# Other constants for the scheduler of an attention-and-retention block: the same work in another order of issue

## The chip, the cores and the metric

The kernel runs on one core of one Trainium2 chip. The metric is the device time of one execution in microseconds. "Before" was executed three times.

## The reference, cut to what matters

One decoder layer on x of 512 x 1024 in float32. The input is normalized and projected by one wide weight matrix. Of the parts, one mixer is sparse attention (8 heads in 2 key groups: a branch on compressed keys, one on selected blocks, one on a window, added with gates), the other is retention with 4 heads in chunks of 128. Both are gated, merged, and go through an output projection; a last normalization and the residual follow.

```python
def compress_blocks(kv, pe, w1, w2):
    ...
    return jax.nn.gelu(flat @ w1) @ w2
...
    kc = compress_blocks(k_cmp_raw, cmp_pe_k, cmp_w1_k, cmp_w2_k)
    vc = compress_blocks(v_cmp_raw, cmp_pe_v, cmp_w1_v, cmp_w2_v)
...
        o = g[..., 0:1] * o_c + g[..., 1:2] * o_s + g[..., 2:3] * o_w
...
    att = jnp.einsum('nihd,njhd->nhij', qc, kc) * decay_mask[None]
    o_inner = jnp.einsum('nhij,njhe->nihe', att, vc)
```

## The kernel before, in words

**Weights and matmuls.** A float32 product is made of three matmuls: every operand is split into a high part (rounded to the type fp32r) and a low part (the rest), and high x high, high x low and low x high are added up in PSUM. Weights come from HBM in loads of 512 KB into four `raw` slots (`load_next`, L442 and L445, on SyncE's queue SP). A co-routine, `splitter`, turns each load into two weight halves: `whi` is a copy on ScalarE (L224) or a cast on VectorE (L232), `wlo` a subtraction on VectorE (L236, in `split_lo`), in a ring of nine. A load can start when both low parts of the slot's former content have been made. L224, L236 and so on are lines of helpers, which record every operation of their kind.

**Stages.** x is transposed and normalized (`hTh`, `hTl`); then come the projections for attention (`tail_a`, `tail_c`, `tail_q`), at about 60 to 80 us the two `hidden` blocks of the key and value compressor with `compress` behind them, then the block Z and the gates, the ZR, QK and VR projections, a `pair` of two such blocks done with seven products in place of eight on sums of weights and of inputs, and the output blocks. Attention (`attention`, `att_unit`, `att_head`, `att_cmp`, `att_sum`, `att_out`) runs between the blocks on all engines: L983 is the fused mask and row maximum of one head and half of the keys' range, ACT takes the exponential behind it, and a transposition on TensorE (L278) and an eviction by ACT and VectorE follow. `zr_end` (L1198) takes a part of ZR out of its PSUM bank.

**Sums of weights.** The seven products need x with signs: `signed` (L608) scales each of eight slices by plus or minus the norm on ACT and stores them to DRAM tiles `s` with 20 DMAs on SP (L621). When all are done, `weight_sums` (L416) lets GpSimd (POOL) copy a `mark` (L419), and then issues six DMAs (four copies, L412, and adds, L410, which read what a copy or a store has written), and nineteen more behind a second `mark` (L423) once the first Z tile is there.

**The order of issue.** Every engine runs its own queue in order, so what stands in front of a slow or waiting instruction matters. The order is worked out when the kernel is built, by the class `Order`. Each piece of work is a co-routine with a priority; it yields the time from which it can go on. `Order` keeps a clock for TensorE (`now`) and one for each other engine, goes through the pieces by priority, and takes the first whose time, plus a hold, has come:

```python
w += LAG + (0.0 if c[0] == MAIN else MARGINS.get(c[3].__name__, MARGIN))
if e:
    w = max(w, self.eng[e] - SLACK)
if w <= self.now:
    best = c
    break
```

The main line (the blocks' matmuls) has the last priority. `MARGINS` (L36) holds, in nanoseconds, each kind of piece back beyond its time: a larger hold lets other pieces and the main line go first. Besides that there are fixed delays: `HOLD` (L732) and `HOLD_C` (L764) between the copies of the keys and their transposition, and `SIGN`, `SIGN_LAG` (L608, L613), the priority of `signed` and the time that it is held. Weight halves have a priority that moves:

```python
return lambda: 0 if p <= wanted[0] + (PSOON if p in pairp else SOON) else 4
```

A half that is needed within the next two (`SOON`), or in the part of the `pair` within `PSOON`, goes before everything, the others behind most of it.

Of the kernel before, what the change touches and what calls it, by code (L numbers as in the profile page):

```python
# [31 lines left out]
MAIN = 9  # L32
LAG, PE_LAG = 55.0, 60.0
TAIL = {"act": 110.0, "dve": 82.0, "pool": 45.0}
MARGIN = 50.0
MARGINS = {'att_cmp': 400.0, 'att_head': 100.0, 'att_out': 100.0, 'att_sum': 20.0, 'att_unit': 100.0, 'compress': 800.0, 'ga_split': 1000.0, 'gates': 1300.0, 'h_sums': 250.0, 'keep': 600.0, 'kept': 1300.0, 'qk_end': 400.0, 'ret': 0.0, 'ret_state': 150.0, 's_early': 1000.0, 's_late': 800.0, 'seven_end': 1000.0, 'split_lo': 100.0, 'splitter': 250.0, 'tail_a': 0.0, 'tail_c': 20.0, 'tail_m': 250.0, 'tail_o': 1300.0, 'tail_q': 20.0, 'tail_qk': 600.0, 'tail_yb': 250.0, 'tail_z': 20.0, 'x_split': 20.0, 'zr_end': 150.0}  # L36
SOON = 2
PSOON = 4
ISSUE = 8.0
SLACK = 700  # L40
WAKE = 7
SIGN, SIGN_LAG = 4, 22000.0
HOLD_C = 1000.0
EARLY = 1300.0
HOLD = 800.0
OSUMS = (1, 0, 0, 0, 1, 0, 0, 0)
FIRST, NEXT, BESIDE = 6, 19, 4000.0
DVE_BIAS = 500
# [2 lines left out]
class Order:  # L51
# [51 lines left out]
    def run(self):  # L103
        while self.cos:
            best = None
            for c in sorted(self.cos, key=lambda c: (c[0]() if callable(c[0]) else c[0], c[1])):
                w, e = c[2] if isinstance(c[2], tuple) else (c[2], None)
                if callable(w):
                    if not w():
                        continue  # L110
                    w = 0.0
                w += LAG + (0.0 if c[0] == MAIN else MARGINS.get(c[3].__name__, MARGIN))
                if e:
# [37 lines left out]
def block_kernel(ctx: ExitStack, tc, x, xT, x0s, ws, small, w2s, norm_post, rope_r, dmask, out):  # L151
# [283 lines left out]
    def load_next():  # L435
        i = len(raws)
        if i < len(loads):
            raw = rp.tile([P, 1024], FT, name="raw", tag="raw", bufs=NR)
            o, c, r = loads[i][0], 0, parts[2 * (i - NR) + 1][2] if i >= NR else 0.0
            for j, n in enumerate(loads[i][1]):  # L440
# [7 lines left out]
                if i + j == 0:  # L448
                    load_xT(0)
            raws.append((raw, e + (EARLY if 6 <= i < 16 else 0.0)))  # L450
            for fn in hook.get(i, ()):
# [66 lines left out]
    def rank(p):  # L518

        return lambda: 0 if p <= wanted[0] + (PSOON if p in pairp else SOON) else 4  # L520

# [61 lines left out]
    def load_xT(k):  # L583
        c0 = 0 if k else 256
        DMA.dma_start(xTf[k][:, c0:], xT[k * P:(k + 1) * P, c0:])
        xTr[k] = od.dma(P * (SEQ - c0) * 4)
# [111 lines left out]
    def keysT(kd, off, br, t, r):  # L698
        ps = yield from PT.get()
        yield r + PE_LAG  # L700
        for g in range(2):
            e = tr(ps[:, g * P:(g + 1) * P], kd[:, off + g * P:off + (g + 1) * P], ident, r)
        yield e, "act"
        v = ps[:, 0:256].rearrange("p (g c a) -> p g a c", g=2, a=2)
        sl = (slice(None), br, slice(None), slice(None), slice(t * 64, (t + 1) * 64))
        e = act(kA[sl], v, r=e)
        yield e, "dve"
        e = sub_split(kB[sl], v, kA[sl], e)
        PT.put(ps, e)
        return e  # L710
# [8 lines left out]
    def tail_a(t, ps, e, ring):  # L719
# [11 lines left out]
        NAT.put(kn, ev)  # L731
        yield e + HOLD  # L732
        yield from keysT(kd, 512, 0, t, e)
# [18 lines left out]
    def tail_c(t, ps, e):  # L752
# [10 lines left out]
        NAT.put(kn, ev)  # L763
        yield e + HOLD_C  # L764
        e = yield from keysT(kd, 0, 1, t, e)
# [1244 lines left out]
```

## Time and profile before

| | |
|---|---|
| median of 3 executions | 496.04 us (494.77 to 496.93) |
| the profiled execution | 496.11 us |
| its span | 494.3 us |
| granted clock of TensorE, mean | 0.994 |
| DMA | 98.75 MB, mean 200 GB/s |
| `raw` loads from the weights' stream | 73, of 512 KB |

The profile has a timeline of every engine (PE is TensorE, PEld its weight loads, DVE VectorE, ACT ScalarE, POOL GpSimd, SP the queue of SyncE). A row of the timeline has the start in us, the duration, engine, line, operation, output <- input, and in brackets the idle time in front and what ended it. A window's row has its length, the busy time of PE, PEld, DVE, ACT and POOL with the number of instructions, the granted clock of TensorE, the busy share of the DMA engines, and GB/s. PE's instructions overlap (a matmul of 512 columns is shown with 0.38 us but the next starts 0.22 behind it), so PE can be busy and still be late.

### The profile page before, as it was taken

What the parts mean: (1) busy time and instruction counts of PE and PEld (TensorE: products, weight loads), DVE (VectorE), ACT (ScalarE), POOL (GpSimd) and SP (SyncE); (2) the same over time, 40 slices, a digit from 0 to 9 for tenths busy, and PEclk for the clock granted to TensorE, in tenths of its full rate; (3) what the DMA queues carried; (4) which work ended last, traced back from release to release, by engine and by line L of the source; (5) the groups of instructions that cost most, each with busy time, mean ns of one, the idle gap of its engine ahead of it and who ended that gap; (6) DMA issues with size and microseconds to landing.
All of it is one profiled execution on the core that took longest, in us unless ns stands there. A gap on an engine that the chain in (4) does not pass through costs nothing.

```text
span 494.3 us, 7886 instructions
## 1 busy us (share of the span) xinstructions
PE 477.7 (97%) x2666; PEld 424.0 (86%) x2666; DVE 424.4 (86%) x996; ACT 323.3 (65%) x722; POOL 39.7 (8%) x66
## 2 busy tenths in 40 slices
PE   8999997999999999999999999999999999999993
PEld 7899876888788888887989878989889999988882
DVE  5789899989989988989798998878787867979886
ACT  5777678677869889983596684665445535538632
POOL 2103010023100210000100000001000000000010
PEclk9999998999999999999999999999999999999998
DMA  8937989779997899426466783630573736535814
GB/s 308 397 141 233 382 227 286 257 138 183 358 286 144 240 368 205 148 64 192 89 195 213 226 256 107 128 129 2 170 253 123 229 119 192 193 127 170 300 42 170
DMA packets 31080, 98.75 MB, mean 200 GB/s; under 512 B 3136, under 2 KB 6976, under 8 KB 30272
## 3 DMA queue, kind: packets, MB, share of 16 engines
q1 hardware_dynamic: 24576, 70.85, 42.7%
q0 software_dynamic: 6320, 27.26, 22.9%
q8 instruction: 21, 0.34, 0.3%
q10 hardware_dynamic: 144, 0.14, 0.1%
q14 instruction: 19, 0.16, 0.1%
HBM read 93.52 MB, written 31.98 MB: 254 GB/s over the span
## 4 chain that ended last, share of the span: by engine, by line
PE 84%; DVE 9%; ACT 2%; issue 2%; DMA 1%; DVEq 0%; POOLq 0%; POOL 0%; ACTq 0%
PE bank L272 67%; PE bank L1251 7%; PE bank L1745 7%; PE bank L278 4%; DVE wlo L236 3%; DVE words L236 2%; DVE arena_r L236 2%; DVE words L983 1%; ACT arena_r L224 1%; DVE words L249 1%; DMA words<-in_x_dram 1%; ACT whi L224 1%; ACT words L224 0%; DVE arena_r L249 0%; DVE whi L232 0%
## 5 line engine op out<-in xcount | busy, mean ns | idle before, releaser
L224 ACT ACTIVATE whi<-raw 128x512 fp32r<-128x512 f32 x175 | 105.3, 626 | 48.6 <-PE bank L272 37.0
L236 DVE TENSOR_TENSOR wlo<-raw,whi 128x512 fp32r<-128x512 f32 x188 | 122.7, 684 | 8.1 <-ACT whi L224 7.4
L272 PE MATMUL bank<-whi,hTh 128*128 128x512 f32 x192 | 72.6, 399 | 3.2 <-DVE arena_r L249 1.9
L272 PE MATMUL bank<-whi,hTl 128*128 128x512 f32 x192 | 69.7, 384 | 0.0
L272 PE MATMUL bank<-wlo,hTh 128*128 128x512 f32 x192 | 69.7, 384 | 0.0
L272 PE MATMUL bank<-arena_r 128*128 128x256 f32 (+2 forms) x328 | 68.2, 330 | 0.7 <-DVE stat L983 0.4
L224 ACT ACTIVATE arena_r<-bank 128x512 fp32r<-128x512 f32 (+3 forms) x104 | 49.2, 476 | 23.1 <-PE bank L278 22.0
L272 PE MATMUL bank<-arena_r,whi 128*128 128x512 f32 (+1 forms) x208 | 61.6, 372 | 0.0
L236 DVE TENSOR_TENSOR arena_r<-bank,arena_r 128x512 fp32r<-128x512 f32 (+3 forms) x104 | 55.8, 541 | 5.3 <-ACT arena_r L224 4.0
L224 ACT ACTIVATE words<-words,stat 128x128 f32<-128x128 f32 (+3 forms) x109 | 56.0, 545 | 6.6 <-DVE stat L236 4.2
L272 PEld LDWEIGHTS bank<-arena_r 128*128 128x128 f32 x328 | 51.7, 191 | 6.6 <-DVE stat L983 1.8
L272 PE MATMUL bank<-hTh,whi 128*128 128x512 f32 (+1 forms) x144 | 51.2, 356 | 0.0
L272 PE MATMUL bank<-hTh,wlo 128*128 128x512 f32 (+1 forms) x144 | 50.1, 348 | 0.9 <-DVE wlo L236 0.9
L272 PE MATMUL bank<-hTl,whi 128*128 128x512 f32 (+1 forms) x144 | 49.9, 347 | 0.0
L272 PEld LDWEIGHTS bank<-whi,hTh 128*128 128x128 f32 x192 | 36.8, 192 | 8.7 <-DVE arena_r L249 2.5
L272 PEld LDWEIGHTS bank<-arena_r,whi 128*128 128x128 f32 x208 | 39.1, 189 | 5.0
L272 PEld LDWEIGHTS bank<-whi,hTl 128*128 128x128 f32 x192 | 36.9, 192 | 5.4
L272 PEld LDWEIGHTS bank<-wlo,hTh 128*128 128x128 f32 x192 | 37.0, 192 | 4.1
L278 PEld LDWEIGHTS bank<-identr,shorts 128*128 128x128 f32 x268 | 30.1, 142 | 8.5 <-ACT words L224 1.7
L272 PE MATMUL bank<-arena_r,wlo 128*128 128x512 f32 x96 | 36.4, 379 | 0.0
L224 ACT ACTIVATE words<-words 128x512 f32<-128x512 f32 (+3 forms) x47 | 27.1, 581 | 10.1 <-DVE words L236 6.4
L278 PE MATMUL bank<-identr,shorts 128*128 128x128 f32 x268 | 32.2, 241 | 1.2 <-ACT words L224 1.0
(182 smaller groups left out, 888.0 us busy)
## 6 DMA issues: line engine op xcount, KB each, us to landing
raw<-in_stream_dram SPq DMA_DIRECT2D x73, 512.0 KB, 4.5
pair<-in_stream_dram POOLq DMA_DIRECT2D x6, 1024.0 KB, 13.7
t<-in_stream_dram POOLq DMA_DIRECT2D x6, 1024.0 KB, 17.5
out<-in_stream_dram POOLq DMA_DIRECT2D x6, 1024.0 KB, 17.1
words<-in_x_dram SPq DMA_DIRECT2D x8, 512.0 KB, 7.3
raw<-s SPq DMA_DIRECT2D x8, 512.0 KB, 3.7
raw<-pair SPq DMA_DIRECT2D x8, 512.0 KB, 4.6
raw<-t SPq DMA_DIRECT2D x8, 512.0 KB, 3.8
```

The source lines that it names most:

```text
L224: S.activation(o, i, func, **kw)
L236: (V if e == "dve" else G).tensor_tensor(o, a, b, op=op)
L249: V.scalar_tensor_tensor(o, a, s, b, op0=op0, op1=op1)
L272: T.matmul(ps, a, b, start=start, stop=stop)
L278: T.transpose(ps, a, idn)
L983: V.tensor_tensor_reduce(pv[:, b, :], sv[:, b, :], maskp[:, 512 - L:512], 1.0, -NEG, OP.add, OP.min, nm[:, b:b + 1])
L1251: T.matmul(ps[m], a, apart(b), start=n in first and s + j == 0, stop=n in last and s + j == 5, skip_group_check=True)
L1745: T.matmul(ps[m], a, apart(b), start=n in first and s + i == 0, stop=n in last and s + i == 5, skip_group_check=True)
```

## The change

The default hold stays (50), and 26 of the 29 holds by kind get other values; `PSOON` goes from 4 to 8, `SIGN` from 4 to 3, `SIGN_LAG` from 22000 to 19000, `HOLD_C` from 1000 to 300 and `HOLD` from 800 to 500. Nothing else is edited. The table in full is one line; of it, the kinds that the text speaks of:

```diff
-MARGINS = {'att_cmp': 400.0, 'att_head': 100.0, 'att_out': 100.0, 'att_sum': 20.0, ... 'compress': 800.0, ... 'gates': 1300.0, ... 'split_lo': 100.0, ... 'tail_c': 20.0, ... 'zr_end': 150.0}
+MARGINS = {'att_cmp': 50.0, 'att_head': 0.0, 'att_out': 1300.0, 'att_sum': 400.0, ... 'compress': 1300.0, ... 'gates': 800.0, ... 'split_lo': 20.0, ... 'tail_c': 250.0, ... 'zr_end': 1700.0}
...
-PSOON = 4
+PSOON = 8
...
-SIGN, SIGN_LAG = 4, 22000.0
-HOLD_C = 1000.0
+SIGN, SIGN_LAG = 3, 19000.0
+HOLD_C = 300
...
-HOLD = 800.0
+HOLD = 500
```

The changed kernel has the same number of matmuls, DMAs and POOL instructions; three copies go from VectorE to ScalarE. Three places of the queues:

VectorE, in the compressor's first `hidden` block. `wlo` is the low part of a weight half, `stat` holds the maxima of the heads, `bank_86` and `bank_87` their scores, and `words_128_...` is the compressor's activation (L983 with `stat` alone reads out the maximum). Before:

```order
L983 ISA words_512_131,stat_905<-bank_87,maskp 128x512
L983 ISA stat_905 128x1
L236 TENSOR_TENSOR words_128_1022<-bank_88,words_128_1023 128x128
L236 TENSOR_TENSOR words_128_1023<-words_128_1022 128x128
L245 TENSOR_SCALAR words_128_1023<-words_128_1023 128x128
L236 TENSOR_TENSOR words_128_1023<-words_128_1023,words_128_1022 128x128
L983 ISA words_512_132,stat_905<-bank_86,maskp 128x512
L983 ISA stat_905 128x1
L983 ISA words_512_133,stat_905<-bank_87,maskp 128x512
L983 ISA stat_905 128x1
L232 CAST whi<-raw 128x512
L236 TENSOR_TENSOR wlo<-raw,whi 128x512 x2
```

In the changed kernel, around the same two heads:

```order
L236 TENSOR_TENSOR wlo<-raw,whi 128x512
L236 TENSOR_TENSOR arena_r<-bank_88,arena_r 64x4x128 x2
L236 TENSOR_TENSOR wlo<-raw,whi 128x512 x2
L243 TENSOR_SCALAR words_512_115<-words_512_115,stat_884 128x512
L236 TENSOR_TENSOR wlo<-raw,whi 128x512
L983 ISA words_512_131,stat_885<-bank_87,maskp 128x512
L983 ISA stat_885 128x1
L983 ISA words_512_132,stat_885<-bank_86,maskp 128x512
L983 ISA stat_885 128x1
L236 TENSOR_TENSOR wlo<-raw,whi 128x512 x3
L236 TENSOR_TENSOR arena_r<-bank_88,arena_r 128x512
L236 TENSOR_TENSOR wlo<-raw,whi 128x512
```

Before, three heads and the activation stand together ahead of the cast and the two splits; now five splits stand ahead of the heads, and the activation comes later.

ScalarE, in `zr_end`, where `words_512_114` takes a quarter of the ZR block out of `bank_85`. Before:

```order
L224 ACTIVATE whi<-raw 128x512 x3
L224 ACTIVATE arena_r<-bank_89 128x4x128
L224 ACTIVATE whi<-raw 128x512 x3
L224 ACTIVATE words_512_114<-bank_85,rs_169 128x512
L224 ACTIVATE whi<-raw 128x512
```

In the changed kernel:

```order
L224 ACTIVATE whi<-raw 128x512 x3
L224 ACTIVATE words_512_129<-words_512_113 128x512
L224 ACTIVATE whi<-raw 128x512
L224 ACTIVATE words_512_114<-bank_85,rs_169 128x512
L224 ACTIVATE whi<-raw 128x512 x2
```

Directly ahead of that eviction stood three copies of weights, and now there stands one; two more have moved behind it.

GpSimd (POOL), where the sums of weights begin. `gate` is the gates' input of one tile of x (`tail_c`), `mark` the copy that waits for the signed x; the rows L412 copy, and the rows L410 add to what the copies and the stores of `s` have left. Before:

```order
L236 TENSOR_TENSOR gate<-words_512_126,cst 128x24
L236 TENSOR_TENSOR gate<-words_512_127,cst 128x24
L236 TENSOR_TENSOR gate<-words_512_126,cst 128x24
L236 TENSOR_TENSOR gate<-words_512_128,cst 128x24
L419 COPY mark<-words_512_115 128x1
L412 DMA pair_157<-in_stream_dram 128x2x1024
```

In the changed kernel:

```order
L236 TENSOR_TENSOR gate<-words_512_126,cst 128x24
L236 TENSOR_TENSOR gate<-words_512_127,cst 128x24
L236 TENSOR_TENSOR gate<-words_512_128,cst 128x24
L419 COPY mark<-words_512_115 128x1
L412 DMA pair_157<-in_stream_dram 128x2x1024
L412 DMA pair_159<-in_stream_dram 128x2x1024
L412 DMA pair_158<-in_stream_dram 128x2x1024
L412 DMA pair_160<-in_stream_dram 128x2x1024
L410 DMA s_148<-s_151 128x2x1024
L410 DMA pair_157<-in_stream_dram 128x2x1024
L236 TENSOR_TENSOR gate<-words_512_126,cst 128x24
```

One of the four rows of `gate` no longer stands ahead of `mark`; it follows two adds. On SP, three loads of weights that stood between the stores of the signed x now follow all of them.

More of the change, by code (lines that the diff above doesn't have):

```diff
@@ L34 @@
 TAIL = {"act": 110.0, "dve": 82.0, "pool": 45.0}
-MARGIN = 50.0
-MARGINS = {'att_cmp': 400.0, 'att_head': 100.0, 'att_out': 100.0, 'att_sum': 20.0, 'att_unit': 100.0, 'compress': 800.0, 'ga_split': 1000.0, 'gates': 1300.0, 'h_sums': 250.0, 'keep': 600.0, 'kept': 1300.0, 'qk_end': 400.0, 'ret': 0.0, 'ret_state': 150.0, 's_early': 1000.0, 's_late': 800.0, 'seven_end': 1000.0, 'split_lo': 100.0, 'splitter': 250.0, 'tail_a': 0.0, 'tail_c': 20.0, 'tail_m': 250.0, 'tail_o': 1300.0, 'tail_q': 20.0, 'tail_qk': 600.0, 'tail_yb': 250.0, 'tail_z': 20.0, 'x_split': 20.0, 'zr_end': 150.0}
+MARGIN = 50
+MARGINS = {'att_cmp': 50.0, 'att_head': 0.0, 'att_out': 1300.0, 'att_sum': 400.0, 'att_unit': 100.0, 'compress': 1300.0, 'ga_split': 1300.0, 'gates': 800.0, 'h_sums': 1000.0, 'keep': 100.0, 'kept': 50.0, 'qk_end': 250.0, 'ret': 20.0, 'ret_state': 0.0, 's_early': 0.0, 's_late': 1000.0, 'seven_end': 0.0, 'split_lo': 20.0, 'splitter': 250.0, 'tail_a': 20.0, 'tail_c': 250.0, 'tail_m': 800.0, 'tail_o': 20.0, 'tail_q': 50.0, 'tail_qk': 600.0, 'tail_yb': 20.0, 'tail_z': 50.0, 'x_split': 0.0, 'zr_end': 1700.0}
 SOON = 2
-PSOON = 4
+PSOON = 8
 ISSUE = 8.0
@@ L41 @@
 WAKE = 7
-SIGN, SIGN_LAG = 4, 22000.0
-HOLD_C = 1000.0
-EARLY = 1300.0
-HOLD = 800.0
+SIGN, SIGN_LAG = 3, 19000.0
+HOLD_C = 300
+EARLY = 1300
+HOLD = 500
 OSUMS = (1, 0, 0, 0, 1, 0, 0, 0)
```

## The prediction

> **What bounds the kernel now.** I read the page first: the busy rows and the chain that ended last.
>
> ```profile
> PE 477.7 (97%) x2666; PEld 424.0 (86%) x2666; DVE 424.4 (86%) x996; ACT 323.3 (65%) x722; POOL 39.7 (8%) x66
> ...
> PE 84%; DVE 9%; ACT 2%; issue 2%; DMA 1%; DVEq 0%; POOLq 0%; POOL 0%; ACTq 0%
> ```
>
> TensorE (PE) is the bound. The change takes no matmul away, so it can win only the 494.3 − 477.7 = 16.6 us in which PE isn't busy and what is hidden in matmuls that sit longer than they need. So I went through the span in windows of 10 us, to see where PE loses time. The six below hold 5.8 of the 16.6; most of the rest is the start and the end, where the order is the same.
>
> ```profile
> 60.00:70.00 10.00, 9.73 (x52) 7.82 (x50) 9.71 (x26) 8.35 (x17) 2.38 (x2) 1.00 0.83 262
> 70.00:80.00 10.00, 7.96 (x48) 6.02 (x47) 9.75 (x26) 7.24 (x15) 0.00 (x0) 1.00 1.06 249
> 80.00:90.00 10.00, 9.19 (x51) 8.14 (x52) 9.93 (x24) 10.00 (x24) 0.00 (x0) 0.83 0.83 303
> ...
> 130.00:140.00 10.00, 9.14 (x48) 7.69 (x47) 9.59 (x24) 7.27 (x14) 2.30 (x2) 1.00 1.03 359
> 220.00:230.00 10.00, 9.07 (x49) 7.31 (x47) 10.00 (x20) 4.74 (x10) 0.00 (x0) 1.00 0.57 190
> 290.00:300.00 10.00, 9.07 (x48) 7.53 (x46) 9.12 (x18) 5.61 (x11) 0.00 (x0) 1.00 0.77 253
> ```
>
> The columns are PE, weight loads, VectorE (DVE), ScalarE (ACT) and POOL busy, then clock, DMA share and GB/s. From 60 to 90 us PE loses 3.1 us by busy time, and in the same stretch DVE is busy for 29.4 of 30: the stage is DVE's. The other three windows lose just under 1 us each. Behind 302 us nothing is left to win: the chain is one run of matmuls.
>
> ```profile
> 349.27 100.83 PE bank L272 x621
> 450.10 33.68 PE bank L1745 x156
> ```
>
> **Term 1, the stage from 60 to 90 us.** PE is in the `hidden` blocks of the compressor here and waits for weight halves; DVE has the first attention heads (L983 head maxima) in its queue as well.
>
> ```profile
> 69.65 1.89 DVE L236 TENSOR_TENSOR wlo<-raw,whi 128x512 fp32r<-128x512 f32 x3
> 71.46 0.68 DVE L983 CUSTOM_DVE_ANT_0 words<-bank,maskp 128x512 f32<-128x512 f32 x1
> ...
> 72.07 1.28 DVE L236 TENSOR_TENSOR wlo<-raw,whi 128x512 fp32r<-128x512 f32 x2
> ...
> 76.42 0.69 DVE L983 CUSTOM_DVE_ANT_0 words<-bank,maskp 128x512 f32<-128x512 f32 x1
> ...
> 79.98 0.42 DVE L232 CAST whi<-raw 128x512 fp32r<-128x512 f32 x1
> 80.44 1.29 DVE L236 TENSOR_TENSOR wlo<-raw,whi 128x512 fp32r<-128x512 f32 x2
> ```
>
> ```profile
> 80.46 0.38 PE L272 MATMUL bank<-whi,arena_r 128*128 128x256 f32 x1 [0.74 <-DVE whi L232]
> 81.18 0.38 PE L272 MATMUL bank<-wlo,arena_r 128*128 128x256 f32 x1 [0.35 <-DVE wlo L236]
> ```
>
> From start to start a split `wlo` takes 0.60 us ((71.46 − 69.65)/3) and a head maximum 0.61 (72.07 − 71.46). Between 76.42 and 79.98 DVE does 3.56 us of work that PE doesn't wait for yet, and PE waits for the cast and the split behind it. These are the rows shown of DVE's order ahead of this text: three heads and the compressor's activation, then the cast and two splits. In the changed order the splits stand ahead, the heads are spread behind them, and the casts that DVE did for `whi` are ACT's. To price this I gave every row of both orders the mean start-to-start time of its form in the trace of before, and compared, for each place where a matmul waits for DVE, the sum of DVE rows up to what it waits for with the sum of PE rows up to the matmul. At the last split of the first `hidden` block that is 73.9 us of DVE against 72.0 of PE before, and 69.1 against 70.2 now. Over the stage the largest lead of DVE's sum falls from 2.95 to 0.30 us. With DVE as full as it is, PE's place moves by that difference, 2.65; the two `whi` waits of the rows above (0.74, and some of the 0.35) go to ACT, which isn't the bound, so I take 3.1 and keep 1.5 to 4.7 (4.7: all of the 3.1 us not busy, and the clock's loss in the rows below, 1.0 in the first and 0.6 in the second).
>
> ```profile
> 82.00:84.00 2.00, 2.00 (x10) 1.71 (x10) 2.00 (x6) 2.00 (x7) 0.00 (x0) 0.50 1.04 424
> 84.00:86.00 2.00, 2.00 (x12) 1.82 (x12) 1.97 (x6) 2.00 (x5) 0.00 (x0) 0.70 0.58 236
> ```
>
> After the thin microseconds from 70 on the granted clock drops to half. I count none of that 1.6 as gain by itself, since DVE's lead covers it: PE at full clock would have waited for DVE. [...]
>
> What ACT needs doesn't rise to the bound: its sum leads PE's by −8.25 us in this stage before and by −7.14 now, and it gets its weights late only if DMA is slow (second rival).
>
> **Terms 2 to 5.** At 132.8 us PE waits for a split that stands behind a chain on the compressed scores.
>
> ```profile
> 131.47 0.68 DVE L249 SCALAR_TENSOR_TENSOR words<-words,words 128x512 f32<-128x512 f32 x1
> 132.07 2.49 DVE L236 TENSOR_TENSOR wlo<-raw,whi 128x512 fp32r<-128x512 f32 x4
> ```
>
> ```profile
> 131.57 0.38 PE L272 MATMUL bank<-hTl,whi 128*128 128x512 f32 x1
> 132.81 0.48 PE L272 MATMUL bank<-hTh,wlo 128*128 128x512 f32 x1 [0.86 <-DVE wlo L236]
> ...
> 293.65 0.48 PE L272 MATMUL bank<-whi,hTh 128*128 128x512 f32 x1 [0.81 <-ACT words L224]
> ```
>
> A matmul of this size takes 33.68/156 = 0.216, so the first loses 132.81 − 131.57 − 0.22 = 1.02, and 0.1 in its own longer row. DVE's lead there is 2.6 before and −1.6 now, from 110 us of PE work to 160: gone, −1.1. The second, at 293.65, waits for an eviction that ACT took late, behind three copies.
>
> ```profile
> 291.36 1.66 ACT L224 ACTIVATE whi<-raw 128x512 fp32r<-128x512 f32 x3
> 292.92 0.68 ACT L224 ACTIVATE words<-bank,rs 128x512 f32<-128x512 f32 x1
> ```
>
> This is the place shown of ACT's order (`words_512_114`). Two copies have moved behind it, 2 × 0.52 (292.92 − 291.36 = 1.56 for three) = 1.04: −1.0. Two more gaps have the shape matmul, ACT, DVE, matmul on one bank, and that stays:
>
> ```profile
> 229.92 0.48 PE L272 MATMUL bank<-whi,hTh 128*128 128x512 f32 x1 [0.76 <-DVE arena_r L249]
> ...
> 301.02 0.48 PE L272 MATMUL bank<-whi,hTh 128*128 128x512 f32 x1 [1.15 <-DVE arena_r L249]
> ```
>
> At the first DVE does another row between, so −0.2; at the second nothing. Against this stand three more changes from matmul to transposition, each worth the 0.08 by which 0.30 exceeds 0.22 here: +0.2.
>
> ```profile
> 102.32 0.38 PE L272 MATMUL bank<-hTh,wlo 128*128 128x512 f32 x1
> 102.62 0.68 PE L272 MATMUL bank<-words,words 128*64 128x64 f32 x8
> ```
>
> And a new order has new short waits; for them I put +0.5, within 0 and 2.5 (two or three of the size of those above).
>
> Sum: −3.1 − 1.1 − 1.0 − 0.2 + 0.2 + 0.5 = −4.7. The profiled execution took 496.11 us, 1.8 over its span, and stands 0.07 above the median 496.04, so no correction: **491.4 us**. What a measurement of this kernel can tell from no change is about 0.5%, 2.5 us.
>
> **The rivals.** First, POOL's queue (slower). One row of `gate` has moved behind the sums of weights on POOL, as its order shows. It now waits until `s` is stored and a copy into `pair_157` has landed, and ACT's `gate<-gate` waits for it, with every `whi` behind.
>
> ```profile
> 42.09 0.54 POOL L236 TENSOR_TENSOR gate<-words,cst 128x24 f32<-128x24 f32 x1 [2.41 <-ACT words L224]
> 44.74 0.19 POOL L419 COPY mark<-words 128x1 f32<-128x1 f32 x1 [2.11 <-ACT words L224]
> 44.87 2.98 POOL L412 DMA_DIRECT2D pair<-in_stream_dram  x4
> 66.08 1.18 POOL L410 DMA_DIRECT2D s<-s  x1 [18.23 <-DMA raw<-in_stream_dram]
> 66.80 1.67 POOL L410 DMA_DIRECT2D pair<-in_stream_dram  x1
> ```
>
> ```profile
> 59.89 0.27 ACT L224 ACTIVATE gate<-gate 128x96 f32<-128x96 f32 x1
> ```
>
> If the two adds come no earlier than before, the gate is done at 66.80 + 1.67 + 0.54 = 69.0, and ACT stands for 9.1 us from 59.89. By the two sums ACT is some 2 us ahead of DVE at the splits that PE waits for, so 7.1 reach PE, and its thinner stretch would bring the 1.6 of the clock onto the path: 491.4 + 8.7 = 500.1. It decides from a gate later than about 62 on, and loses to before from about 66.6. Against it: the signed copies on ACT come some 4 us earlier, their stores stand ahead of the loads on SP, and `mark` with them comes at about 40, so the copy should land near 54. [...] I give this 0.11.
>
> Second, transfers (no change). With the sums running, loads are slow:
>
> ```profile
> 46.00:66.00 20.00, 19.79 (x110) 17.00 (x109) 17.06 (x45) 12.79 (x24) 1.85 (x3) 1.00 1.03 377
> ...
> 68.00:84.00 16.00, 12.95 (x74) 9.89 (x72) 15.69 (x41) 12.74 (x30) 0.46 (x1) 0.93 1.03 265
> ```
>
> ```profile
> raw<-in_stream_dram SPq DMA_DIRECT2D x3, 512.0 KB, 9.8
> ```
>
> The last row is of the loads issued from 70 to 76 us. In the new order a load has about 5 us from its free slot to ACT's first use, where it had 8 to 12. At 9.8 ACT slips by some 4 us and term 1 is gone: 491.4 + 3.1 = 494.5. Whether it happens turns on the sums being through by 68 us: 20 + 16 us of full engines, less the stores that are done earlier (some 3.5) and the loads of 70 to 84 (some 6), from 40 on, is 66.5. That is close, and I give it 0.22.
>
> Third, the new waits eat all but term 1's lower bound, or one stall of 2 to 3 us opens that I didn't find: 494 to 497, 0.08.
>
> **How the numbers follow.** The forecast has 0.59: its own range is 488.0 to 493.5 (below: term 1 at 4.7, no new waits, and 1.3 of the two gaps that I let stay; above: term 1 at 1.5, new waits at 1). The second rival, 0.22, lies at 493 to 496, of which 0.05 is under 493.5. POOL's queue, 0.11, lies mostly above 498.5. Faster by over 0.5% (under 493.6): 0.59 + 0.05 = 0.64; slower (over 498.5): 0.11; within: 0.25. The range of 488.0 to 497.0 leaves out the rival of POOL and a few hundredths at either end.
>
> **What would show it.** Right: 70 to 80 us with PE busy over 8.8, the clock at 1.00 from 82 to 86, no `whi<-DVE` wait near 80, no wait of 0.8 for `wlo` near 128 and none for `words` near 288, the gap of 1.15 still there near 296. Wrong: ACT idle ahead of `gate<-gate` with POOL as releaser (first rival), ACT idle ahead of `whi` with `raw` as releaser between 68 and 85 (second), or PE behind 302 us with waits that it doesn't have now.

## The result, and the profile after

| | before | changed |
|---|---|---|
| median | 495.40 us (494.45 to 496.93, 4 runs) | 490.12 us (489.33 to 491.13, 4 runs) |
| ratio, 95% interval | | 0.9899 (0.9877 to 0.9921) |
| the profiled execution, its span | 496.11, 494.3 us | 489.62, 487.8 us |

The forecast was 491.4 us in 488.0 to 497.0. All medians, here and below, leave out two executions of the experiments, one of e10 with 812.73 and one of e11 with 2029.06 us. The page of the changed kernel, its busy rows and its chain:

```profile
PE 473.0 (97%) x2666; PEld 421.2 (86%) x2666; DVE 422.1 (87%) x993; ACT 323.4 (66%) x725; POOL 38.9 (8%) x66
...
PE 82%; ACT 6%; DVE 6%; DMA 3%; issue 2%; SPq 1%; POOLq 0%; POOL 0%; DVEq 0%; ACTq 0%
```

DVE's share of the chain falls from 9 to 6%, and ACT's rises from 2 to 6%. The windows that answer to those of before, in the same columns:

```profile
60.00:70.00 10.00, 9.84 (x57) 8.52 (x56) 9.77 (x25) 9.87 (x22) 0.00 (x0) 1.00 1.03 252
70.00:80.00 10.00, 7.86 (x52) 6.58 (x53) 9.86 (x20) 9.94 (x21) 0.00 (x0) 1.00 0.76 234
80.00:90.00 10.00, 9.65 (x53) 7.68 (x52) 9.90 (x22) 7.78 (x17) 0.00 (x0) 1.00 0.92 295
...
130.00:140.00 10.00, 10.00 (x60) 9.04 (x60) 9.57 (x25) 6.82 (x16) 0.00 (x0) 1.00 1.06 279
220.00:230.00 10.00, 8.99 (x48) 7.56 (x47) 7.99 (x17) 3.64 (x8) 0.00 (x0) 1.00 0.50 158
290.00:300.00 10.00, 8.85 (x49) 7.77 (x48) 9.28 (x21) 4.28 (x9) 0.00 (x0) 1.00 0.41 131
```

The window from 130 us is full now and the clock from 80 is at 1.00. But from 70 to 80 PE isn't busier than before (7.86 against 7.96), and ACT is full from 60 to 80. The windows are fixed in time while the work has moved in them, so they don't show what a stage has gained. For that I took the lateness of PE: the start of a matmul less the PE rows ahead of it in the order, each with the steady start-to-start time of its form. Where it grows, PE loses time. Both kernels are read at the same amounts of PE work, so the growth between two places can be compared:

| place, in us of PE work | lateness before | changed | difference of growth |
|---|---|---|---|
| 10 | 4.59 | 3.15 | −1.44 |
| 55 | 6.16 | 4.28 | −0.44 |
| 90 (the stage of 60 to 90 us) | 16.35 | 11.58 | −2.89 |
| 110 | 17.23 | 12.87 | +0.41 |
| 120 (the wait at 132.8) | 18.51 | 12.88 | −1.27 |
| 200 | 21.41 | 16.06 | +0.28 |
| 268 (with the gap at 229.9) | 24.06 | 18.52 | −0.19 |
| 270 (the wait at 293.65) | 25.13 | 18.63 | −0.96 |
| the last matmul | 28.02 | 21.50 | −0.02 |

The sum is −6.52, of which the first 1.44 isn't the change's: the order up to there is the same (last section). The others make −5.08, and the medians differ by 5.28. The waits of PE from 30 to 345 us, in total, number and the longest:

```profile
PE bank L272 <- DVE wlo L236: 2.4, 4, 1.4
PE bank L272 <- DVE arena_r L249: 2.2, 2, 1.2
PE bank L278 <- DVE words L236: 0.3, 1, 0.3
```

The two of `arena_r` are the gaps at 229.92 and 301.02 of before (1.01 and 1.15 us idle now, 0.76 and 1.15 then); those for `whi` of DVE and `words` of ACT are gone. POOL's timeline, the place of the first rival:

```profile
37.32 0.23 POOL L236 TENSOR_TENSOR gate<-words,cst 128x24 f32<-128x24 f32 x1 [2.54 <-ACT words L224]
38.40 0.18 POOL L419 COPY mark<-words 128x1 f32<-128x1 f32 x1 [0.84 <-ACT words L224]
38.52 2.98 POOL L412 DMA_DIRECT2D pair<-in_stream_dram  x4
41.49 1.21 POOL L410 DMA_DIRECT2D s<-s  x1
45.66 1.18 POOL L410 DMA_DIRECT2D pair<-in_stream_dram  x1 [2.96 <-DMA pair<-in_stream_dram]
46.39 0.73 POOL L236 TENSOR_TENSOR gate<-words,cst 128x24 f32<-128x24 f32 x1
```

```profile
58.47 0.27 ACT L224 ACTIVATE gate<-gate 128x96 f32<-128x96 f32 x1
```

The copies start 6.4 us earlier, the adds at 41.5 and 45.7 in place of 66, and the moved gate is done 11 us ahead of ACT's need. The place of the second rival, the loads issued from 68 to 76 us:

```profile
raw<-in_stream_dram SPq DMA_DIRECT2D x4, 512.0 KB, 4.4
```

They land in 4.4 us, where the three of before took 9.8. The engines were free for them only just in time: the second add, issued at 45.66, took 24.1 us, so it landed at 69.8.

```profile
pair<-in_stream_dram POOLq DMA_DIRECT2D x1, 1024.0 KB, 24.1
```

### The profile page after: what moved, and what is told of

It is laid out like the page before. It is cut to its first block, busy times and chain, and to the rows that moved or that the text cites. A ratio compares the mean times of both kernels' runs of the same rounds, so it can differ in the third digit from the quotient of the medians.

```text
span 487.8 us, 7885 instructions
## 1 busy us (share of the span) xinstructions
PE 473.0 (97%) x2666; PEld 421.2 (86%) x2666; DVE 422.1 (87%) x993; ACT 323.4 (66%) x725; POOL 38.9 (8%) x66
## 4 chain that ended last, share of the span: by engine, by line
PE 82%; ACT 6%; DVE 6%; DMA 3%; issue 2%; SPq 1%; POOLq 0%; POOL 0%; DVEq 0%; ACTq 0%
PE bank L272 70%; PE bank L1251 7%; PE bank L278 4%; ACT whi L224 3%; ACT words L224 2%; DMA raw<-in_stream_dram 2%; DVE wlo L236 2%; DMA words<-in_xT_dram 1%; DVE words L236 1%; DVE words L249 1%; ACT arena_r L224 1%; DVE arena_r L236 1%; ACT rsrow L224 0%; DVE hTl L236 0%; DVE arena_r L249 0%
## 5 line engine op out<-in xcount | busy, mean ns | idle before, releaser
L224 ACT ACTIVATE words<-words,stat 128x384 f32<-128x384 f32 (+3 forms) x112 | 57.2, 542 | 3.2 <-DVE stat L983 2.0
```

What stands on the lines that cost most here:

```text
L224: S.activation(o, i, func, **kw)
```

## The experiments

Three theories stood against each other. **A**, the prediction's: how much DVE work stands ahead of what PE waits for sets the stage of 60 to 90 us. **B**: the sums of weights are through before the stage's loads, whatever the order. **C**, from the chain in the changed kernel: ACT bounds the stage now. By that chain, the share of each engine and line from 58 to 84 us:

```profile
by line: ACT whi L224 37.4%; ACT words L224 33.9%; issue 11.6%; ACT arena_r L224 10.2%; PE bank L272 6.6%; PE bank L278 1.2%
```

All results first. "Stage" is the growth of lateness from 55 to 76 us of PE work, "copies" the start of the first four copies on POOL, "loads" the median time of the loads issued from 68 to 76 us.

| kernel | median | ratio to before, 95% interval | stage, us | copies | loads, us |
|---|---|---|---|---|---|
| before | | | 9.3 | 44.87 | 9.8 |
| changed | 490.12 | 0.9899 (0.9877 to 0.9921) | 6.6 | 38.52 | 4.4 |
| e1, signs alone | 495.72 | 0.9995 (0.9973 to 1.0017) | 5.7 | 38.21 | 3.5 |
| e2, holds alone | 502.99 | 1.0141 (1.0103 to 1.0179) | 9.4 | 43.35 | 9.5 |
| e3, sums late | 494.96 | 1.0004 (0.9983 to 1.0026) | 11.6 | 46.44 | 9.8 |
| e4, `zr_end` old | 492.03 | 0.9928 (0.9903 to 0.9954) | 6.6 | 38.77 | 4.5 |
| e5, before, adds late | 501.54 | 1.0099 (1.0063 to 1.0134) | 9.0 | 44.97 | 4.2 |
| e6, changed, adds late | 490.16 | 0.9869 (0.9833 to 0.9905) | 6.5 | 39.23 | 4.4 |
| e7, ACT plus 3.6 | 492.59 | 0.9932 (0.9906 to 0.9958) | 9.3 | 38.62 | 4.2 |
| e8, DVE plus 3.7 | 493.83 | 0.9944 (0.9919 to 0.9969) | 10.2 | 39.06 | 3.2 |
| e9, gate late | 506.51 | 1.0202 (1.0161 to 1.0242) | 23.7 | 38.48 | none issued |
| e10, sums half as late | 494.03 | 0.9957 (0.9933 to 0.9981) | 10.5 | 42.12 | 8.3 |
| e11, casts on DVE | 491.66 | 0.9914 (0.9887 to 0.9941) | 8.1 | 38.75 | 4.3 |
| e12, head hold 100 | 495.39 | 0.9985 (0.9955 to 1.0014) | 6.5 | 38.65 | 4.6 |

Before's median was 495.25 us beside e1 to e4, 495.73 beside e5 to e8 and 495.51 beside e9 to e12, so a difference of medians between such groups is good to some 0.5 us. The stage column comes from one trace of each kernel. It can be read more closely: in the eight traces with the changed kernel's order on PE (the changed kernel, e3 and e6 to e11) the lateness behind 90 us of PE work grows by 9.9 to 10.1 us in every one.

**Parts of the change: e1 and e2.** In e1 the kernel before gets two constants:

```diff
-SIGN, SIGN_LAG = 4, 22000.0
+SIGN, SIGN_LAG = 3, 19000.0
```

> The kernel before with SIGN and SIGN_LAG alone changed. In its order the largest lead of DVE's sum over PE's from 60 to 90 us is 0.3 us (before 2.95, changed 0.3), from 110 to 130 it is -1.9 (before 2.75), and the eviction in zr_end still stands behind eight copies of weights. Theory A (the prediction's: how much DVE work stands ahead sets PE's place): -3.1 for the stage and -1.1 for the wait near 132.8, nothing in zr_end: -4.2 us against before, a ratio near 0.9915. Theory B (the earlier sums leave the DMA engines free when the weights of the stage are loaded): -3.1 for the stage as well, since the sums come early here too, and the wait near 132.8 stays: ratio near 0.9937. Rival: the gain needs the table of holds, and this one moves less than 1 us: ratio above 0.998.

The stage gained 3.6 us (5.7 against 9.3), as A and B have it, and the kernel gained nothing. The wait near 132.8 went too, as A has it and B doesn't: from 110 to 120 us of PE work the lateness grows by 0.3, and by 1.3 in before. What was won was lost elsewhere: against before, 1.4 us between 10 and 55, 0.9 between 160 and 180, and more behind 277. The waits of e1's PE over the whole execution:

```profile
PE bank L278 <- ACT words L224: 4.4, 3, 2.1
PE bank L272 <- DVE wlo L236: 1.9, 4, 0.6
PE bank L278 <- DVE arena_r L236: 1.1, 1, 1.1
```

The three waits for ACT's `words` (one at 296.20 us with 1.57 idle) and that for `arena_r` aren't in the changed kernel: e1's lateness grows by 3.7 from 277 us of PE work on, where the changed kernel's grows by 1.3. In e2 the kernel before gets the table of holds and nothing else:

```diff
-MARGINS = {'att_cmp': 400.0, ... 'zr_end': 150.0}
+MARGINS = {'att_cmp': 50.0, ... 'zr_end': 1700.0}
```

> The kernel before with the table MARGINS alone changed; signed x and sums of weights as late as before. The largest lead of DVE's sum from 60 to 90 us is 1.9 (before 2.95), from 110 to 130 it is -1.6. Theory A: -1.0 for the stage, -1.1 near 132.8: -2.1 us, ratio near 0.9958, loads of the stage still taking some 8 to 10 us. Theory B: nothing for the stage, since the sums are as late as before; at most -1.1: ratio near 0.998.

It is 1.4% slower. The stage gains nothing (9.4), as B has it, though DVE's lead is 1.9 in place of 2.95: the loads took 9.5 us. And there are new waits behind, the longest here:

```profile
295.94 0.74 PE L272 MATMUL bank<-whi,hTh 128*128 128x512 f32 x1 [2.08 <-ACT words L224]
```

Neither part is worth anything alone. The gain of the stage comes with the signs; the places behind it are in order in the changed kernel, which has both and the new values of `PSOON`, `HOLD` and `HOLD_C` as well. What these three contribute wasn't tried.

**When the sums run: e3, e10, e5, e6.** In e3 POOL is kept busy ahead of the mark with a tile that nobody reads, so every other queue keeps the changed kernel's order:

```diff
+        for _ in range(32):
+            G.memset(idle, 0.0)
         G.tensor_copy(mark, last[0])
```

> The changed kernel with 32 empty fills of a spare tile on POOL ahead of the mark, so that the sums of weights start some 6 us later (near 44.9, as before) while the order on PE, DVE and ACT is the changed kernel's. Theory A: no difference to the changed kernel, ratio to before near 0.990. Theory B: the loads from 68 to 76 us take 8 to 10 us again, ACT waits for raw, and the 3.1 us of the stage are lost: ratio near 0.996.

B is right, and the price is larger than either theory had: the stage takes 11.6 us, 5.0 more than in the changed kernel and 2.3 more than before, and the whole gain is gone. ACT waits for the loads:

```profile
72.48 1.15 ACT L224 ACTIVATE whi<-raw 128x512 fp32r<-128x512 f32 x2 [2.69 <-DMA raw<-in_stream_dram]
73.54 1.18 ACT L224 ACTIVATE arena_r<-bank 64x512 fp32r<-64x512 f32 x2
76.67 1.15 ACT L224 ACTIVATE whi<-raw 128x512 fp32r<-128x512 f32 x2 [1.96 <-DMA raw<-in_stream_dram]
```

e10 has 16 fills in place of 32.

> As e3, with 16 empty fills in place of 32: the sums start some 4 us later than in the changed kernel (e3: 8). The prediction's sum of DMA work has the engines free at about 66.5 us and the first load of the stage wanted at 69, so there are some 2.5 us to spare. If so, 4 us cost 1 to 2 us: ratio near 0.993. If the loads follow the sums in proportion (e3: 5 us for 8), 2.5 us: ratio 0.995. If there is a threshold above 4 us: nothing, ratio 0.990.

The copies start 3.6 us later than in the changed kernel, the loads take 8.3 us, and the stage takes 3.9 more. So there were no 2.5 us to spare, and the loss follows the delay nearly one to one at first (3.9 for 3.6) and then less (5.0 for 7.9). The opposite case is e5: the kernel before, with the two adds taken out of the stage.

```diff
+            if issued[0] in (4, 5):
+                held.append((o, a))
...
         G.tensor_copy(mark, szn[:, 0, 0:1])
+        for o, a in held:
+            G.dma_start(o, a, accum_op=OP.add)
```

> The kernel before, every queue in its order, but the first two adds of the sums of weights (s and pair) stand behind the second mark on POOL, near 100 us, and not at 66 us. So the DMA engines are free when the loads from 70 to 76 us run, and nothing else is changed. Theory B (it is the transfers, whatever the order): the loads take 4 us, and the stage from 60 to 90 us gains as it did in the changed kernel, some 2 to 3 us: ratio near 0.995. Theory A (in the order before it is the DVE queue; loads have 8 to 12 us to spare and are never waited for): no gain, ratio 1.000, PE still waits for wlo and whi of DVE.

A is right for the stage: with loads of 4.2 us, the order of before still takes 9.0 (9.3), and PE still waits for DVE's cast and split:

```profile
80.20 0.38 PE L272 MATMUL bank<-whi,arena_r 128*128 128x256 f32 x1 [0.74 <-DVE whi L232]
80.93 0.38 PE L272 MATMUL bank<-wlo,arena_r 128*128 128x256 f32 x1 [0.35 <-DVE wlo L236]
```

The 1% that the kernel lost is from a place that I hadn't thought of. The chain of sums runs some 16 us later to its end, its last adds are issued at 191.77 and 196.54, and they meet the rope table's load there, which takes 11.4 us (2.6 in before) and for which DVE and then PE wait:

```profile
DVE words L249 <- DMA words<-in_rope_r_dram: 6.3, 1, 6.3
```

```profile
PE bank L278 <- DVE arena_r L236: 5.0, 1, 5.0
```

e6 is the same edit in the changed kernel.

> The changed kernel with the same two adds behind the second mark, every other queue in its order. After e3, where the sums came late and the loads cost 5 us, this shows whether the loads still cost anything in the changed kernel. If its sums are through in time (theory A with the loads as its condition): the loads go from 4.4 to about 3.5 us and the time stays within 0.5 us of the changed kernel, ratio to before 0.989 to 0.990. If they still hold ACT up: 1 us or more faster, ratio 0.988 or below. The moved gate row comes earlier here too, and shouldn't matter.

The time is the changed kernel's (490.16 against 490.12) and so is the stage (6.5). Its ratio has a wider interval, which holds the changed kernel's 0.9899. The loads still take 4.4 us, and not the 3.5 that I expected. So the two adds cost the changed kernel nothing; what shorter loads would be worth isn't shown by this run.

**Which engine bounds the stage: e7, e8, e11.** e7 does seven copies of weight halves twice on ACT, e8 head maxima twice on DVE, both in the changed kernel:

```diff
+                    if 24 <= p < 31:
+                        S.activation(vh, src, AF.Copy)
```

> The changed kernel with seven copies whi<-raw done twice on ACT (halves 24 to 30, in the first hidden block): 7 x 0.52 = 3.6 us more on ACT between 60 and 75 us. Theory A as predicted (DVE bounds the stage, ACT has some 2 us to spare): 0 to 1.6 us slower than the changed kernel, ratio to before 0.990 to 0.993. Theory C (in the changed kernel ACT bounds the stage, as the chain of its profile has it): 3 to 3.6 us slower, ratio 0.996 to 0.997.

```diff
+            if len(heads) <= 6:
+                V.tensor_tensor_reduce(pv[:, b, :], sv[:, b, :], maskp[:, 512 - L:512], 1.0, -NEG, OP.add, OP.min,
+                                       nm[:, b:b + 1])
```

> The changed kernel with the first six head maxima (L983) done twice on DVE: 6 x 0.61 = 3.7 us more on DVE between 60 and 80 us. Theory A: 3 to 3.7 us slower than the changed kernel, ratio to before 0.996 to 0.997. Theory C (ACT bounds the stage): 0 to 1.6 us slower, since DVE has its own wait for whi to fill, ratio 0.990 to 0.993.

The edit of e8 doubles five heads and not six, since the sixth finds more than six in the list by the time its maximum is issued (the trace has 69 maxima, the changed kernel's 64). But a pair takes 1.35 us (69.69 − 68.34 in the rows below) where one takes 0.61, so five make 3.7 us all the same. These 3.7 us on DVE cost the stage 3.6; 3.6 us on ACT cost 2.7. So DVE has nothing to spare and ACT 0.9, where the prediction had 2. A holds for DVE and C is nearly right too: the two are within 1 us of each other, and the chain, which went to 82% over ACT, names one of them. In e8 PE waits for DVE at the doubled work itself:

```profile
68.34 0.70 PE L272 MATMUL bank<-arena_r 128*128 128x512 f32 x2 [1.09 <-DVE stat L986]
69.69 0.70 PE L272 MATMUL bank<-arena_r 128*128 128x512 f32 x2 [0.42 <-DVE stat L986]
72.24 0.70 PE L272 MATMUL bank<-arena_r 128*128 128x512 f32 x2 [0.74 <-DVE stat L986]
```

e11 gives DVE back the five casts that it did before:

```diff
+                    if p in (25, 31, 34, 36, 38):
+                        V.tensor_copy(vh, src)
```

> The changed kernel with the five copies of weights that DVE cast before (halves 25, 31, 34, 36, 38 of the hidden blocks) cast on DVE again, at the same places of the order: 5 x 0.34 = 1.7 us more on DVE, 2.6 less on ACT between 60 and 80 us. After e8 (3.7 us more on DVE cost 3.7) and e7 (3.6 more on ACT cost 2.5): theory A says 1.0 to 1.7 us slower than the changed kernel, ratio near 0.993. If ACT bounds the stage it is faster, ratio below 0.989.

The stage takes 1.5 us more, and the kernel's median is 1.5 us longer, though the intervals of the two ratios overlap. With loads equally fast (4.2 to 4.4 us) the stage takes 9.0 in before's order (e5), 8.1 in the changed order with the casts back on DVE, and 6.6 in the changed order. So more than half of the stage's gain is that ACT does these casts, and the rest, 0.9, is the other changes of the order.

**The places behind: e4 and e12.** e4 is the changed kernel with `zr_end` back at 150, e12 with `att_head` back at 100.

```diff
-'zr_end': 1700.0
+'zr_end': 150.0
```

> The changed kernel with the hold of zr_end at its old value, 150. The eviction into words_512_114 stands behind five copies of weights again. Theory A: the wait of PE for ACT's words near 287 us is back with 0.8 us idle, and the kernel is 1.0 us slower than the changed one: ratio to before near 0.992. Rival: the eviction before was late because DVE released its slot late (its last row there ended at 291.9, one copy ahead of the eviction), so the five copies are done in time and no wait comes back: ratio near 0.990.

Slower by 1.9 in the medians, with ratios whose intervals overlap, and by 1.1 in the two profiles, about as A has it, but not at its place. The wait at 287 us doesn't come back: ACT takes the eviction at 286.38, 1.0 later than the changed kernel (285.38), and PE doesn't wait. The next bank is late instead, the one that was to stay at 1.15:

```profile
295.19 0.48 PE L272 MATMUL bank<-whi,hTh 128*128 128x512 f32 x1 [1.93 <-DVE arena_r L249]
```

```diff
-'att_head': 0.0
+'att_head': 100.0
```

> The changed kernel with the hold of att_head at its old value 100 (changed: 0). By the two sums DVE's largest lead from 60 to 90 us falls from 0.3 to -0.2 and ACT's from -7.1 to -7.8, and both stay lower up to 200 us. Theory A: 0.5 us faster than the changed kernel, ratio to before 0.988 to 0.989, if no new short waits come behind 130 us. If the lead is not all that counts there (e1 lost later what it had gained), no gain or some us slower: ratio 0.990 to 0.995.

The stage gains 0.1 (6.5) where the lead has 0.5, and the kernel is 5 us slower. From 265 to 277 us of PE work its lateness grows by 6.3, where the changed kernel's grows by 1.7. Two of the waits there:

```profile
288.63 0.48 PE L272 MATMUL bank<-whi,hTh 128*128 128x512 f32 x1 [0.41 <-ACT words L224]
297.34 0.54 PE L278 MATMUL bank<-identr,shorts 128*128 128x128 f32 x4 [1.57 <-ACT words L224]
```

By the expectation DVE's and ACT's sums are lower than the changed kernel's up to 200 us, so they gave no sign of this. The sums compare what has been done, and a short turn of matmul, ACT, DVE and matmul on one bank isn't in them.

**The price of the first rival: e9.** 100 fills between the adds and the gate.

```diff
+        if issued[0] == 6:
+            for _ in range(100):
+                G.memset(idle, 0.0)
         tt(gate[:, t, :], kn[:, 256:280], bg, OP.add, e, "pool")
```

> The price of the prediction's first rival: the changed kernel with 100 empty fills of a spare tile on POOL between the two adds and the moved gate row, which then runs near 66 us in place of 46.4; all other queues in their order. By the prediction ACT would stand from 58.5 to about 67, some 2 us of it to spare and 1.6 us of the clock on top: 6.5 + 1.6 = 8 us slower than the changed kernel, ratio to before near 1.005. With the 1 us to spare that e7 showed: 7.5 to 9. Rival: the wait falls into a stretch where PE waits for DVE anyway, and less than 4 us of it show, ratio below 0.998.

```profile
47.66 26.67 POOL L761 MEMSET idle<- 128x128 f32 x100
74.31 0.22 POOL L236 TENSOR_TENSOR gate<-words,cst 128x24 f32<-128x24 f32 x1
```

```profile
74.56 0.28 ACT L224 ACTIVATE gate<-gate 128x96 f32<-128x96 f32 x1 [16.02 <-POOL gate L236]
```

The fills took 0.27 us each and not 0.2, so the gate was 8 us later than meant and ACT stood for 16.0. The kernel is 16.4 us slower than the changed one; the prediction's formula gives 16.0 − 2 + 1.6 = 15.6. The mechanism and its price in sum are right, though the two corrections, the 2 and the 1.6, weren't measured apart; it just didn't happen, since the adds come 20 us earlier.

## Why the prediction was right

**Term 1, the stage**, −3.1: measured −2.89 from 55 to 90 us of PE work. Its reason, DVE's queue, holds: in the changed order DVE has nothing to spare (e8), and in before's order PE still waits for DVE when the loads are fast (e5). The lead of 2.65 is a sum of all DVE rows, so it holds the casts already, as 5 × 0.34 = 1.7 us of DVE's time by e11's estimate; e11 gives 1.5 for them. The 0.45 that I put on top for the waits on `whi` counts them a second time, and without it the term would have been 0.2 too small in place of 0.2 too large. A condition of it was in the second rival only: the new order has no slack for the loads, and 3.6 us of delay in the sums would have taken it all (e10). I gave this 0.22 and priced it at 3.1; e3 shows 5.0. My sum of DMA work was also too short: it has the engines free at 66.5 with a start at 40, and they were free at 69.8 with a start at 38.5. That the rival stayed away is in part luck: the sums started 1.5 us earlier than I had worked out, and by e10 a start as much later as that would have cost about 1.6 (an estimate from its 3.9 for 3.6).

**The sign in the window was wrong.** I wanted PE over 8.8 busy from 70 to 80 us, and it is 7.86. The loss has moved into this window, since the stage comes earlier; from 80 to 90 it is 9.65. The clock was at 1.00 from 82 to 86, as forecast.

**The clock** was rightly given no gain of its own. The changed kernel has no half speed (a granted clock of 0.5) in the stage, and e6 has 3.4 us of it, but both take the same time there, 6.6 and 6.5 us. This is e6's window, with a clock of 0.87:

```profile
70.00:80.00 10.00, 8.10 (x49) 6.91 (x49) 9.82 (x23) 9.94 (x21) 0.00 (x0) 0.87 0.74 238
```

**ACT isn't the bound** was true by 0.9 us, not 2 (e7; that run also had half speed from 74.8 to 81.6 us, so the 0.9 could be somewhat more).

**The wait at 132.8**, −1.1: measured −1.27. Its `wlo` is made ahead now: the splits stand in one run of five.

```profile
124.56 3.10 DVE L236 TENSOR_TENSOR wlo<-raw,whi 128x512 fp32r<-128x512 f32 x5
127.57 0.69 DVE L249 SCALAR_TENSOR_TENSOR words<-words,words 128x512 f32<-128x512 f32 x1
```

**The wait at 293.65**, −1.0: measured −0.96, and the eviction is early (285.38, the matmul that follows on its bank at 286.80). That two copies fewer ahead of it are the cause isn't shown: with five copies ahead (e4) the wait stayed away. By the expectation of e4, the row of DVE that the slot waits for ended at 291.9 in before, and in the changed kernel DVE is earlier; which of the two counted I didn't separate.

**The gap at 229.92**, −0.2: measured −0.07, and not by the step that I forecast, a shorter turn of the bank: the idle time at that matmul grew from 0.76 to 1.01. **The gap at 301.02** stayed, at 1.15. **Transpositions and new waits**, +0.7: measured +0.11, the rest of the table (−0.44, +0.41, +0.28, −0.12 without the gap, −0.02). So the sum of −4.7 met −5.08 with errors of at most 0.6 in a term.

What the prediction didn't price is how easily the places behind 140 us go wrong. e1, e2 and e12 lose some 4, 11 and 5 us more there than the changed kernel, and the sums gave no sign of it. I went through the turns of a bank at two places only; the +0.5 stood for all others, and was lucky beside e12's 5.

## What to carry to other kernels

Sum the work ordered ahead of each wait on the engine that is full, and compare the two orders: here that gave the stage's gain within 0.3 us. But do it for the loads as well, since this order, without slack, paid 3.9 us for sums that started 3.6 us later (e10). Behind the stage go through each short turn of a bank by itself: the sums don't see it, and it is where a single hold cost 5 us. Constants of such a scheduler have to be tried together: here some of them alone gave 0.0% (e1) and 1.4% slower (e2), and all of them 1.0% faster.

## What was not expected of the hardware

The start differs. In the profile before, the first matmuls run at half pace until 10.16 us, in the changed kernel until 5.67, with the same order. Rows of before and of the changed kernel, four matmuls of 512 columns each:

```profile
6.78 1.91 PE L272 MATMUL bank<-whi,hTl 128*128 128x512 f32 x4
8.49 1.84 PE L272 MATMUL bank<-wlo,hTh 128*128 128x512 f32 x4
```

```profile
6.10 1.03 PE L272 MATMUL bank<-whi,hTl 128*128 128x512 f32 x4
6.96 1.03 PE L272 MATMUL bank<-wlo,hTh 128*128 128x512 f32 x4
```

Four take 1.71 us in one and 0.86 in the other, so 0.43 us a matmul against 0.22. That is also the pace that before has at a granted clock of 0.50, where two matmuls of 512 columns take 0.85 us:

```profile
82.59 1.06 PE L272 MATMUL bank<-arena_r 128*128 128x512 f32 x2
83.44 0.67 PE L278 MATMUL bank<-identr,shorts 128*128 128x128 f32 x4
```

The trace's record of the clock begins with full speed at 10.12 us in before and at 5.55 in the changed kernel, and the windows' column has 1.00 ahead of that only because nothing is recorded there. So I take the slow start for the clock, an inference from these times. The order up to there is the same, and its first twelve matmuls of 512 columns take 5.24 us in before (4.92 to 10.16) and 3.08 in the changed kernel (4.75 to 7.83), so the 1.44 by which the lateness differs at 10 us of PE work has nothing to do with the change. Two profiles should be compared from behind the start.

In before the clock fell while TensorE still worked: it was at 0.50 from 81.80 us on, for 3.41 us. In the 8 us from 74 to 82 PE was busy for 5.16, and its longest idle time there was the 0.74 ahead of 80.46.

```profile
74.00:76.00 2.00, 1.00 (x8) 0.80 (x7) 1.96 (x4) 0.66 (x2) 0.00 (x0) 1.00 1.09 281
76.00:78.00 2.00, 1.58 (x9) 1.00 (x8) 1.90 (x9) 1.52 (x3) 0.00 (x0) 1.00 1.04 260
78.00:80.00 2.00, 1.39 (x10) 0.98 (x9) 1.93 (x8) 2.00 (x5) 0.00 (x0) 1.00 1.06 279
80.00:82.00 2.00, 1.19 (x6) 0.92 (x7) 1.97 (x6) 2.00 (x6) 0.00 (x0) 0.95 1.00 315
```

A thin stretch isn't always followed by a fall: in the changed kernel PE was busy for 2.39 of the 4 us from 72 to 76, and the clock stayed at 1.00 up to the end of PE's work. What decides between the two isn't shown.

Beside the adds in DRAM the throughput was lower than beside the copies: in before, the engines were busy for 1.03 of the time at 265 GB/s from 68 to 84 us, where adds run, and for 1.03 at 377 from 46 to 66, where the copies run. Beside either, loads of 512 KB took long: 9.8 us beside the adds at 70 us in before, 11.5 near 200 in e5, and 13.6 beside the copies, issued at 48 in before. Where the copies started by 39.3 us, or the first two adds were held back (e5, e6), the loads of the stage took 3.2 to 4.6 us.
